# Attention beside a stream of projections: each block's values one block later, right behind the next block's turned weights

## The chip, the cores and the metric

The kernel runs on one core of a Trainium2 chip. The metric is device microseconds of one execution of the whole program; a figure for a kernel is the median over several executions. A profiled execution gives a trace as well, in which "span" is the time from the first to the last instruction of the program.

## What is computed

One layer of a hybrid trunk for 512 latent and 128 context tokens, 1024 features wide: a gated feed-forward half-step, then token mixing (differential attention beside a chunked recurrent memory), then a second feed-forward half-step, each under modulated norms. The change lies in the attention. Cut to that:

```python
def diff_attention(q, k, v, lam):          # 8 heads, blocks of 128 queries
    s = einsum('bqhcd,bkhcd->bhcqk', qi, kf) * scale     # c: two score maps per head
    pr = softmax(s, axis=-1)
    w = pr[:, :, 0] - lam * pr[:, :, 1]
    return einsum('bhqk,bkhv->bqhv', w, vf)              # then a norm per head
```

The four blocks of latent queries see 768 keys (512 latent, 256 cached); the one block of context queries sees its own 128.

## The kernel before

All weights and activations are 32-bit floats. The large products are made of three matmuls each, on operands split into a high and a low part (`mm3`). The program is built with a scheduler that orders the instructions of each engine at build time by its own estimates, unless the code pins them: matmuls and transposes always keep the order of the program (`mm` and `tr`, lines 74 to 78), and what stands under `with written():` (line 69) keeps its order on VectorE and ScalarE among what is pinned. Other instructions of VectorE and ScalarE are placed between the pinned ones by the scheduler.

The attention loop (lines 1961 to 2025) goes over 8 heads and, in each, over 5 blocks of 128 queries (`qi` 0 to 4; block 4 is the context's). Two things share TensorE there. One is the attention itself. The other is a queue of projection work (`fill`): units of 24 matmuls that belong to the memory branch or to later heads, of which the table `UNITS` (line 1954) gives each block one or two, and each head's end some more. Heads 0 and 1 mostly have two per block, the later heads mostly one. A unit's result is evacuated from PSUM by ScalarE (in some cases VectorE), unpinned. For the weights of a unit, ScalarE makes the high part (`fill.ahead`, pinned at the end of a block) and VectorE the low part (`fill.low`, pinned behind the scores' minimum).

A block consists of these steps, all pinned:

- `scores` (line 1597): up to eight matmuls into the one place for scores (`sc`, three PSUM banks, one buffer), then on VectorE the minimum of each row (`mn`, line 1617); queries carry a minus sign, so this is the soft-max's maximum.
- `soft` (line 1620): on ScalarE the exponentials of both maps, with their sums (`p0`, `p1`, `sm`). When they are read, the place for scores is free for the next block.
- `mix` (line 1628): on VectorE the reciprocals of the sums (`rc`, line 1631), a factor `r`, and the mixed weights, written over `p0` (in the profile `p<-p,r,p`).
- `turn` (line 1636): TensorE transposes of the mixed weights (`ps_wT`, six, or one in block 4), copied to SBUF (`wT`, two buffers) by ScalarE.
- `values` (line 1648): the product of the turned weights and the values (`ps_o`: twelve matmul instructions, two in block 4), evacuated by VectorE with the reciprocal as its scale (`ao`, line 1656).

`mn`, `sm`, `rc` and `wT` have two buffers each, and `p1` one. The other PSUM tiles (`ps_wT`, `ps_o`, the units' `ps_t` and `ps_p`, the turned queries and keys `ps_qkT`) share five banks. The order in a block is: scores of this block, turn of the block before, exponentials of this block, low part, first unit, mix of this block, values of the block before, second unit if there is one, high part. Behind the fifth block the head's end has turn 4, the turning of the next head's queries, units, values 4, the head's norm, and the turning of the next head's keys. Between the blocks the scheduler places what the unpinned parts leave on VectorE, above all the norm and rotation of the projected queries and keys for the next pair of heads (`qk_norm_rope`, line 1470: `rope`, `q_tok`, `k_tok` in the profile), which falls into the odd heads.

Of the kernel before, what the change touches and what calls it, by code (L numbers as in the profile page):

```python
# [7 lines left out]
F32 = mybir.dt.float32  # L8
# [23 lines left out]
def tile_trunk(ctx: ExitStack, tc: tile.TileContext, a: dict):  # L32
# [4 lines left out]
    def placed(ins):  # L37
        if as_written[0] is in_row:
            i = ins.ins
            if i.engine in in_row:  # L40
                tc.add_manual_dep(
                    i, in_row[i.engine].name, mybir.DependencyInfo(mybir.DependencyClass.NoSync, mybir.DependencyReason.DATA),
                    reason="written",
                )
            in_row[i.engine] = i
        elif as_written[0]:
            tc.keep_in_program_order(ins)
        return ins
# [19 lines left out]
    @contextmanager  # L68
    def written():
        was, as_written[0] = as_written[0], in_row  # L70
        yield
        as_written[0] = was

    def mm(*args, **kw):
        tc.keep_in_program_order(nc.tensor.matmul(*args, **kw))  # L75
# [1467 lines left out]
    class Head:  # L1543
# [53 lines left out]
        def scores(self, qi):  # L1597
            s = ps_s.tile([128, 1536], F32, tag="sc", name="sc")
            qs = slice(qi * 128, (qi + 1) * 128)
            qT, kH, kL = self.qT, self.kH, self.kL  # L1600
            for c in range(2):
                if qi < 4:
                    for k0, k1 in (((0, 512), (512, 768)) if c == 0 else ((0, 256), (256, 768))):
                        o = s[:, c * 768 + k0 : c * 768 + k1]
                        mm(o, qT[:, c, qs], kH[:, c, k0:k1], start=True, stop=False)
                        mm(o, qT[:, c, qs], kL[:, c, k0:k1], start=False, stop=True)
                else:

                    o = s[:, c * 512 : c * 512 + 256].rearrange("p (c t) -> p c t", c=2)
                    mm(o, qT[:, c, qs], kH[:, :, 768:896], start=True, stop=False)  # L1610
                    mm(o, qT[:, c, qs], kL[:, :, 768:896], start=False, stop=True)
            if qi < 4:
                sv = s.rearrange("p (c t) -> p c t", c=2)
            else:
                sv = s[:, 0:1280].rearrange("p (c t) -> p c t", c=2)[:, :, 0:128]
            mn, sm, rc = (ap.tile([128, 2], F32, tag=n, name=n, bufs=2) for n in ("mn", "sm", "rc"))
            placed(vec.tensor_reduce(out=mn, in_=sv, axis=AX.X, op=ALU.min))  # L1617
            self.s[qi] = sv, 768 if qi < 4 else 128, mn, sm, rc

# [66 lines left out]
    def begin_pools():  # L1686
        gates.close()
        in_pools["k"] = ctx.enter_context(tc.tile_pool(name="mlk", bufs=1, side="right"))
        in_pools["q"] = queries_of.enter_context(tc.tile_pool(name="mlq", bufs=1, side="right"))
# [21 lines left out]
    def load_memory(h):  # L1711
        for box, tag, src in ((mqT, "q", mq_dram), (mkT, "k", mk_dram)):
            box[h] = pair(tag, h, f"m{tag}T")
            nc.sync.dma_start(out=box[h], in_=src[:, 2 * h : 2 * h + 2, :])
# [209 lines left out]
    ap = att.enter_context(tc.tile_pool(name="att", bufs=1, reuse_waits="tile"))  # L1924
# [16 lines left out]
    def aside(hd, qi, part):  # L1941
        if hd == 0:
            for _ in range(ROWS.get((qi, part), 0)):
                next(rows, None)
        if part == 0:
            with written():
                fill.low()
        if part == 1 and hd == 1 and qi in (1, 2):
            gate_load(qi - 1)
        if part == 0 and hd == 1 and qi in (2, 3):  # L1950
            gate_cols()
# [9 lines left out]
    for hd in range(8):  # L1961
        H = heads[hd]
        odd = hd % 2
        for qi in range(5):
            n = UNITS[hd][qi]
            with written():
                H.scores(qi)
                if qi > 0:
                    H.turn(qi - 1)
                H.soft(qi)  # L1970
            aside(hd, qi, 0)
            fill.units(n[0])
            with written():
                H.mix(qi)
            if late is not None:
                late()
                late = None
            if qi > 0:
                with written():
                    H.values(qi - 1)  # L1980
            if qi == 3 and hd < 7:
                with written():
                    heads[hd + 1].pack()
            aside(hd, qi, 1)
            if (hd, qi) == (0, 2):
                begin_pools()
            elif (hd, qi) == (1, 0):
                load_memory(0)
            fill.units(n[1])
            with written():  # L1990
                fill.ahead()
        n = UNITS[hd][-1]
        with written():
            H.turn(4)
        if hd < 7:
            N = heads[hd + 1]
            N.queries()
            fill.units(n[0])
            with written():
                H.values(4)  # L2000
            H.finish_norm()
            if odd:
                for i in range(5):
                    fill.one()
                    if i in (0, 1):
                        N.keys(i)
                    if i == 1:
                        with written():
                            fill.ahead()
            else:  # L2010
                N.keys(0)
                fill.units(n[1])
                N.keys(1)
                with written():
                    fill.ahead()
                fill.units(n[2])
            late = H.finish
        else:
            fill.eager = True
            fill.units(1)  # L2020
            H.values(4)
            H.finish_norm()
            fill.drain(3)
            with written():
                H.finish()
# [511 lines left out]
def build(nc, shapes):  # L2537
    a = {}
    for n, s in shapes.items():
        a[n] = nc.dram_tensor("in_" + n, s, F32, kind="ExternalInput").ap()  # L2540
    for n, s in _OUTS.items():
        a[n] = nc.dram_tensor("out_" + n, s, F32, kind="ExternalOutput").ap()
    with tile.TileContext(nc, schedule_with_timeline_sim=True) as tc:
        tile_trunk(tc, a)
# [21 lines left out]
```

## Time and profile before

| | |
|---|---|
| median of 3 executions | 1815.26 us (1815.12 to 1816.54) |
| the profiled execution | 1815.7 us, span 1813.9 us |
| TensorE busy | 1785.6 us (98%) |
| VectorE busy | 1349.6 us (74%) |
| ScalarE busy | 910.8 us (50%) |
| attention loop, first scores to last values | 683.8 to 1071.0 us of the span |
| moved from and to HBM | 240.49 MB read, 68.87 MB written |

In the profile PE is TensorE (PEld its weight loads), DVE VectorE, ACT ScalarE, SP the queue that issues most DMAs. A row of the order of time has the start in us from the span's start, the duration in us, the engine, the line of the code, the operation, and what it writes and reads; at its end, in brackets, the idle time of the engine before it and what ended that. A row of the waits has who waited for whom, the total in us, how many times and the longest. A row of a stretch has its bounds and its length, the busy time of PE, PEld, DVE, ACT and POOL with their instructions, the granted clock of TensorE as a share of full speed, the share of the DMA engines and their GB/s. Matmuls are pipelined, and the end that a row gives for them overlaps the next one's start; the distance between two starts is what one costs.

### The profile page before, as it was taken

Reading aid. Unit: us, or ns where it says so; the run is one execution under the profiler, and the core shown is the slowest. Engines: PE = TensorE matmul, PEld = TensorE weight load, DVE = VectorE, ACT = ScalarE, POOL = GpSimd, SP = SyncE. Lnnn points to the kernel's source line nnn. Section 1 sums busy time; section 2 is a strip of 40 time slices with the busy share of each in tenths; the row PEclk is TensorE's granted clock in tenths of the full one; section 3 lists DMA queues with packets and bytes.
Section 4 is the critical chain, followed back from the end, with each engine's and each line's share of the span. In section 5 each row is a group of like instructions: output and inputs, shape, how many; then the busy total and the mean of one; then the engine's idle time right before and its main releaser. Section 6 shows DMA issues by size and latency. Waiting matters only on the chain.

```text
span 1813.9 us, 30780 instructions
## 1 busy us (share of the span) xinstructions
PE 1785.6 (98%) x12550; PEld 1744.6 (96%) x12550; DVE 1349.6 (74%) x2178; ACT 910.8 (50%) x1588; POOL 39.2 (2%) x69
## 2 busy tenths in 40 slices
PE   8999999999999999999999999999999999999998
PEld 6999999999999999999999998899999999999998
DVE  6879987677888765858584557977767888897485
ACT  5654544333655445556564547674336545554432
POOL 0000000100000000000000000000000000000010
PEclk9999999999999999999999999999999999999999
DMA  8355566977245434221221124576642355557992
GB/s 326 111 198 171 186 236 221 350 227 266 83 139 181 160 131 143 78 69 63 69 69 55 68 81 163 182 257 218 221 171 80 134 173 185 203 180 274 353 311 80
DMA packets 132207, 311.36 MB, mean 172 GB/s; under 512 B 10017, under 2 KB 93217, under 8 KB 119009
## 3 DMA queue, kind: packets, MB, share of 16 engines
q1 hardware_dynamic: 121122, 265.22, 42.3%
q0 software_dynamic: 10256, 41.55, 7.1%
q8 instruction: 98, 1.61, 0.4%
q10 hardware_dynamic: 688, 2.63, 0.4%
q14 instruction: 43, 0.35, 0.1%
HBM read 240.49 MB, written 68.87 MB: 171 GB/s over the span
## 4 chain that ended last, share of the span: by engine, by line
PE 85%; DVE 7%; DMA 4%; ACT 2%; issue 1%; SPq 0%; DVEq 0%; ACTq 0%
PE ps_f L75 48%; PE ps_p L75 14%; PE ps_t L75 12%; PE sc L75 2%; PE ps_n L75 2%; PE ps_o L75 2%; DVE ww L54 2%; PE ps_u L75 1%; DMA raw_a<-in_w_ada_k 1%; PE ps_wT L78 1%; PE ps_qkT L78 1%; DMA raw<-in_w2b 1%; DVE junk L814 1%; DMA P<-nm_dram 1%; DVE mn L1617 1%
## 5 line engine op out<-in xcount | busy, mean ns | idle before, releaser
L75 PE MATMUL ps_f<-S,ww 128*128 128x320 f32 x2400 | 387.5, 310 | 5.2 <-DVE ww L54 1.9
L75 PEld LDWEIGHTS ps_f<-S,ww 128*128 128x128 f32 x2400 | 359.8, 188 | 9.6 <-DVE ww L54 6.5
L54 DVE TENSOR_TENSOR ww<-raw,ww 128x2048 fp32r<-128x2048 f32 (+1 forms) x73 | 163.9, 2246 | 74.3 <-ACT ww L51 74.2
L75 PE MATMUL ps_t<-wH,hH 128*128 128x256 f32 x640 | 185.7, 290 | 0.9 <-DVE x L57 0.9
L75 PE MATMUL ps_f<-hm,ww 128*128 128x320 f32 x1176 | 185.8, 309 | 0.1
L75 PE MATMUL ps_t<-wH,hL 128*128 128x256 f32 x640 | 181.6, 284 | 0.9 <-DVE hL L54 0.9
L75 PE MATMUL ps_t<-wL,hH 128*128 128x256 f32 x640 | 181.4, 283 | 0.0
L75 PEld LDWEIGHTS ps_f<-hm,ww 128*128 128x128 f32 x1176 | 175.7, 188 | 0.6 <-DVE ww L54 0.6
L51 ACT ACTIVATE ww<-raw 128x2048 fp32r<-128x2048 f32 (+1 forms) x73 | 136.9, 1875 | 60.3 <-DVE raw L54 33.0
L54 DVE TENSOR_TENSOR raw<-raw 128x1024 f32<-128x1024 f32 x186 | 161.0, 865 | 2.2
L75 PE MATMUL ps_f<-hm,wB 128*128 128x320 f32 x1008 | 161.5, 309 | 0.0
L75 PE MATMUL ps_p<-hH,wH 128*128 128x320 f32 x480 | 151.1, 315 | 0.7 <-ACT aT L51 0.7
L75 PEld LDWEIGHTS ps_f<-hm,wB 128*128 128x128 f32 x1008 | 151.3, 188 | 0.0
L75 PE MATMUL ps_p<-hH,wL 128*128 128x320 f32 x480 | 148.3, 309 | 0.0
L75 PE MATMUL ps_p<-hL,wH 128*128 128x320 f32 x480 | 148.3, 309 | 0.0
L51 ACT ACTIVATE u<-ps_f 128x320 f32<-128x320 f32 x129 | 55.8, 433 | 161.5 <-PE ps_f L75 159.7
L75 PEld LDWEIGHTS ps_t<-wH,hH 128*128 128x128 f32 x640 | 123.0, 192 | 1.5 <-ACT nsq L51 1.1
L75 PEld LDWEIGHTS ps_t<-wH,hL 128*128 128x128 f32 x640 | 122.9, 192 | 1.1 <-DVE hL L54 1.1
L75 PEld LDWEIGHTS ps_t<-wL,hH 128*128 128x128 f32 x640 | 123.1, 192 | 0.4
L1617 DVE TENSOR_REDUCE mn<-sc 128x2 f32<-128x1536 f32 (+1 forms) x40 | 59.5, 1489 | 56.0 <-PE sc L75 55.8
L54 DVE TENSOR_TENSOR wB<-raw,wB 128x1024 fp32r<-128x1024 f32 x64 | 78.1, 1221 | 26.7 <-ACT wB L51 26.7
L51 ACT ACTIVATE wH<-raw 128x2048 fp32r<-128x2048 f32 (+1 forms) x45 | 75.4, 1681 | 42.2 <-PE ps_p L75 35.5
(309 smaller groups left out, 3621.9 us busy)
## 6 DMA issues: line engine op xcount, KB each, us to landing
g_dram<-g SPq DMA_DIRECT2D x44, 640.0 KB, 7.6
raw_a<-in_w_ada_c POOLq DMA_DIRECT2D x35, 512.0 KB, 4.7
g_dram<-g SPq DMA_DIRECT2D x24, 480.0 KB, 8.1
raw<-in_w1b SPq DMA_DIRECT2D x11, 1024.0 KB, 4.9
raw<-in_w3b SPq DMA_DIRECT2D x11, 1024.0 KB, 6.3
raw<-in_w1a SPq DMA_DIRECT2D x10, 1024.0 KB, 4.9
raw<-in_w3a SPq DMA_DIRECT2D x10, 1024.0 KB, 6.2
hm<-g_dram SPq DMA_DIRECT2D x7, 1280.0 KB, 12.5
```

Source lines behind the costliest of these rows:

```text
L51: return placed(nc.scalar.activation(*args, **kw))
L54: return placed(eng.tensor_tensor(out=out, in0=in0, in1=in1, op=op))
L75: tc.keep_in_program_order(nc.tensor.matmul(*args, **kw))
L78: tc.keep_in_program_order(nc.tensor.transpose(*args, **kw))
L814: placed(vec.tensor_tensor_reduce(out=junk, in0=raw, in1=self.csil[:, v, :], op0=ALU.mult, op1=ALU.add, scale=1.0, scalar=0.0, accum_out=m ...
L1617: placed(vec.tensor_reduce(out=mn, in_=sv, axis=AX.X, op=ALU.min))
```

## The change

Values move from behind the mix to right behind the turn, and one block further on. In block q the turn is that of block q-1, as before, and the values are now those of block q-2, and they stand ahead of the exponentials in the code, ahead of the first unit on TensorE, and ahead of the low part and the mix on VectorE. Blocks 0 and 1 have no values; the head's end has two: values 3 right behind turn 4, and values 4 where they were. `rc` gets a third buffer, because a block's reciprocals are still to be read when those of the second block after it get their place. Nothing else is changed.

```diff
@@ -1613,7 +1613,7 @@
-            mn, sm, rc = (ap.tile([128, 2], F32, tag=n, name=n, bufs=2) for n in ("mn", "sm", "rc"))
+            mn, sm, rc = (ap.tile([128, 2], F32, tag=n, name=n, bufs=b) for n, b in (("mn", 2), ("sm", 2), ("rc", 3)))
@@ -1967,6 +1967,8 @@
                 H.scores(qi)
                 if qi > 0:
                     H.turn(qi - 1)
+                if qi > 1:
+                    H.values(qi - 2)
                 H.soft(qi)
             aside(hd, qi, 0)
             fill.units(n[0])
@@ -1975,9 +1977,6 @@
             if late is not None:
                 late()
                 late = None
-            if qi > 0:
-                with written():
-                    H.values(qi - 1)
             if qi == 3 and hd < 7:
                 with written():
                     heads[hd + 1].pack()
@@ -1992,6 +1991,7 @@
         n = UNITS[hd][-1]
         with written():
             H.turn(4)
+            H.values(3)
         if hd < 7:
             N = heads[hd + 1]
             N.queries()
```

## The prediction

> **What bounds the kernel now.** I read the page's first part, then the waits of TensorE alone in the attention stage (683.8 to 1071.0 us of the span), then the order of time in the blocks whose order changes.
>
> ```profile
> span 1813.9 us, 30780 instructions
> ...
> PE 1785.6 (98%) x12550; PEld 1744.6 (96%) x12550; DVE 1349.6 (74%) x2178; ACT 910.8 (50%) x1588; POOL 39.2 (2%) x69
> ```
>
> ```profile
> 683.80:1071.00 387.20, 382.05 (x3043) 371.98 (x3042) 251.16 (x387) 215.27 (x454) 0.00 (x0) 1.00 0.22 74
> ```
>
> ```profile
> PE ps_wT L78 <- DVE p L57: 3.0, 7, 0.8
> PE sc L75 <- ACT p L51: 1.6, 3, 0.9
> PE ps_o L75 <- ACT wT L51: 0.5, 1, 0.5
> ```
>
> The second fence is the attention stage: length, then the busy time of TensorE, its weight loads, VectorE, ScalarE. The third is all that TensorE waits for there (total, times, longest). TensorE is the bound, in program order; of 387.2 us it idles 5.1. So an order that removes no TensorE work can win only out of those 5.1, and any cover that it takes from a wait shows in the time at once. Two of the three waits are the soft-max chain: the turn of a block waits for its mixed weights (`p`, DVE L57), and the next scores wait until the exponentials (ACT) have read the one place for scores. Only the third concerns the values.
>
> **What the change moves.** No instruction is added or removed. Between the scores of block q and the turn of q, TensorE had: turn q-1, a unit of the projections, values q-1, scores q+1. Afterwards it has turn q-1, values q-2, the unit, scores q+1. For q from 2 on that is the same amount of cover, and block 0 never had values. For q = 1 there is no q-2: twelve matmuls of cover go, and they come back behind turn 4, where the head's end has units and turned queries to spare. So the price lies in the second block of each head. Head 2, its second block:
>
> ```profile
> 799.64 0.20 ACT L51 ACTIVATION_READ_ACCUMULATOR p<-sc,mn 128x1 f32 x1
> ...
> 799.89 0.50 PE L75 MATMUL sc<-kH,qT 128*128 128x512 f32 x1 [0.34 <-ACT p L51]
> ...
> 801.40 0.87 PE L78 MATMUL ps_wT<-ident,p 128*128 128x128 f32 x6
> ...
> 802.03 0.36 PE L75 MATMUL ps_t<-wH,hH 128*128 128x256 f32 x1
> ...
> 804.99 1.50 PE L75 MATMUL ps_o<-v_tok,wT 128*128 128x128 f32 x12
> 805.08 0.20 ACT L51 ACTIVATION_READ_ACCUMULATOR p<-sc,mn 128x1 f32 x1
> ...
> 805.93 1.02 DVE L57 SCALAR_TENSOR_TENSOR p<-p,r,p 128x768 f32<-128x768 f32 x1
> 806.25 0.47 PE L75 MATMUL sc<-kH,qT 128*128 128x512 f32 x1
> ...
> 807.73 0.82 PE L78 MATMUL ps_wT<-ident,p 128*128 128x128 f32 x6
> ```
>
> The values' twelve matmuls hold TensorE from 804.99 to 806.25: **1.26 us**. Without them the scores of block 2 want to start at 804.99, but the exponentials are read out at 805.08 + 0.20 = 805.28; the rows at 799.64 and 799.89 show scores starting 0.05 behind such an end, so 805.33. From there scores to turn takes 801.40 - 799.89 = 1.51 (that case too began with a wait): 806.84. The mixed weights end at 805.93 + 1.02 = 806.95, and the turn follows an end of the mix by 0.05 (head 3 below: 851.36 + 1.02 = 852.38, turn at 852.43): 807.00. Free of waits the turn would come at 807.73 - 1.26 = 806.47. Lost: **0.53**. In short: the new turn is at the mix's end + 0.05, the old turn less 1.26 is what it should be. Heads 4, 6 and 7, mix and old turn:
>
> ```profile
> 900.26 1.02 DVE L57 SCALAR_TENSOR_TENSOR p<-p,r,p 128x768 f32<-128x768 f32 x1
> ...
> 902.08 0.81 PE L78 MATMUL ps_wT<-ident,p 128*128 128x128 f32 x6
> ...
> 1000.47 1.02 DVE L57 SCALAR_TENSOR_TENSOR p<-p,r,p 128x768 f32<-128x768 f32 x1
> ...
> 1002.21 0.82 PE L78 MATMUL ps_wT<-ident,p 128*128 128x128 f32 x6
> ...
> 1048.96 1.02 DVE L57 SCALAR_TENSOR_TENSOR p<-p,r,p 128x768 f32<-128x768 f32 x1
> ...
> 1050.85 0.82 PE L78 MATMUL ps_wT<-ident,p 128*128 128x128 f32 x6
> ```
>
> Head 4: 901.33 against 900.82, **0.51**. Head 6: 1001.54 against 1000.95, **0.59**. Head 7: 1050.03 against 1049.59, **0.44**. Heads 0 and 1 run two units in this block; one unit is 804.99 - 802.03 = 2.96 more cover, so nothing is lost. In heads 3 and 5 the turn waits for the mix already:
>
> ```profile
> 849.12 1.48 DVE L1475 TENSOR_REDUCE ss<-rope 128x20 f32<-128x1280 f32 x1
> ...
> 851.36 1.02 DVE L57 SCALAR_TENSOR_TENSOR p<-p,r,p 128x768 f32<-128x768 f32 x1
> ...
> 852.43 0.87 PE L78 MATMUL ps_wT<-ident,p 128*128 128x128 f32 x6 [0.31 <-DVE p L57]
> ...
> 943.83 0.23 ACT L51 ACTIVATION_READ_ACCUMULATOR p<-sc,mn 128x1 f32 x1
> ...
> 944.16 0.47 PE L75 MATMUL sc<-kH,qT 128*128 128x512 f32 x1
> ...
> 946.24 0.34 DVE L61 TENSOR_SCALAR ao<-ps_o,rc 128x128 f32<-128x128 f32 x1
> 946.38 0.87 PE L78 MATMUL ps_wT<-ident,p 128*128 128x128 f32 x6 [0.58 <-DVE p L57]
> 946.50 0.17 DVE L57 SCALAR_TENSOR_TENSOR rt<-ry 128x20 f32<-128x20 f32 x1
> ...
> 958.61 0.17 DVE L1631 RECIPROCAL rc<-sm 128x2 f32<-128x2 f32 x1 [1.33 <-ACT p L51]
> ```
>
> Nothing there ends the mix earlier, so the whole **1.26** is lost in each. Sum of the second blocks: 0.53 + 0.51 + 0.59 + 0.44 + 2 x 1.26 = **4.59**.
>
> VectorE's order changes as well: the evacuation `ao` stood behind the mix, now it stands behind the scores' minimum and ahead of the weights' low part (`fill.low`) and the mix; the wait that it adds is for the moved values, and low part, reciprocals and mix are queued behind it. Where no low part follows, VectorE would wait for the exponentials then anyway, and `ao` costs nothing; where one follows, the mix is late, which matters only where it is tight, in head 7, block 3:
>
> ```profile
> 1057.76 0.82 PE L78 MATMUL ps_wT<-ident,p 128*128 128x128 f32 x6
> ...
> 1059.63 2.28 DVE L54 TENSOR_TENSOR wL<-raw,wH 128x2048 fp32r<-128x2048 f32 x1
> ...
> 1061.94 1.50 PE L75 MATMUL ps_o<-v_tok,wT 128*128 128x128 f32 x12
> ...
> 1062.28 1.02 DVE L57 SCALAR_TENSOR_TENSOR p<-p,r,p 128x768 f32<-128x768 f32 x1
> ...
> 1063.47 0.35 DVE L61 TENSOR_SCALAR ao<-ps_o,rc 128x128 f32<-128x128 f32 x1 [0.17 <-PE ps_o L75]
> ...
> 1063.74 0.82 PE L78 MATMUL ps_wT<-ident,p 128*128 128x128 f32 x6
> ```
>
> `ao` starts 1.53 behind its first matmul (1061.94 to 1063.47). The turn before it, at 1057.76, takes 0.63 (801.40 to 802.03), so `ao` comes at 1059.92 and the low part at about 1060.2, 0.57 late; the mix ends at 1063.87, the turn at 1063.92 in place of 1063.74: **0.18**. For the other side, in heads 3 and 5 VectorE works almost without a break, and `ao` takes 0.26 there between mix and next minimum (946.24 to 946.50). One of these now falls where VectorE sat idle (1.33 ahead of 958.61). Bounds: nothing, or 0.35 in each of three blocks of both heads, 2.1; I take 0.26 in each head, **-0.5**, the nearer to a VectorE that is full.
>
> The values' own wait (0.5, in head 7's last block) goes, but the next instruction, turn 4, waits for its mix regardless: nothing. The third place for `rc` is the condition of the order, not a cost: its 8 bytes live one block longer. No DMA is issued in the moved lines; in SP's queue nothing changes place. POOL has no instruction here.
>
> Sum: 4.59 + 0.18 - 0.5 = **4.3 us**. The profiled execution took 1815.7 (span 1813.9 and 1.8 around it), so 1820.0 on its footing; it stood 0.4 over the median of 1815.26, so on the median's footing **1819.6 us**, 0.24% more.
>
> **Rivals.** *VectorE's order is dealt anew (not slower).* The rotation of the next heads' queries and keys isn't pinned; its place in VectorE's stream is chosen when the program is built. In heads 3 and 5 the 1.48 us reduction at 849.12 stands ahead of the mix. If it goes behind it, the mixes end up to 1.48 earlier, and the exponentials bound these blocks: in head 5 the scores start at 943.83 + 0.23 + 0.05 = 944.11 and the turn 1.51 later, 945.62 against 946.38 - 1.26 = 945.12, a loss of 0.5; as much in head 3 at most, 1.0 together in place of 2.52. With such slack the late waits of head 5 go too:
>
> ```profile
> 958.63 0.39 PE L75 MATMUL sc<-kH,qT 128*128 128x256 f32 x1 [0.90 <-ACT p L51]
> ...
> 960.14 1.26 PE L78 MATMUL ps_wT<-ident,p 128*128 128x128 f32 x6 [0.78 <-DVE p L57]
> ```
>
> ```profile
> 957.06:960.47 3.41, 1.73 (x13) 1.34 (x13) 2.01 (x6) 3.41 (x8) 0.00 (x0) 1.00 0.12 38
> 960.47:963.88 3.41, 3.41 (x18) 3.41 (x17) 2.28 (x6) 2.07 (x7) 0.00 (x0) 0.50 0.00 0
> ```
>
> The column before the DMA share is the granted clock: after a stretch with TensorE busy for 1.73 of 3.41 it was 0.50 for 3.41 us, which costs half of that, 1.7. Gain: 1.48 of the 0.90 + 0.78, and 1.7. Total 2.07 + 1.0 + 0.18 - 0.5 - 1.48 - 1.7 = -0.4: **1814.8**, no change that can be measured. It decides from mixes over 1 us earlier. For it: the order is open. Against: the minima and mixes are pinned, and the reduction was ready early. Chance 0.18.
>
> *The clock drops (slower).* In the second blocks of heads 3 and 5 the new idle time and the old lie within some 3.5 us: for head 5, 944.11 less 942.90 (944.16 - 1.26) ahead of the scores, 1.21, and 946.38 - 945.62 = 0.76 ahead of the turn, 2.0 in all; as the rows show, TensorE idled 1.7 ahead of 960.47. Two more half-rate stretches give 4.3 + 3.4: **1823.0**. The chance, 0.12, is small because it hangs on where a stretch begins. The Trainium skill (TensorE: Matmul & The Clock Gate, Part 1) has the half rate come only after a whole idle window of about 3.4 us; by that rule this rival is out and the sum stays 4.3. The trace does not agree: no wait ahead of 960.47 is over 0.90.
>
> *The head's end pays back.* The values behind turn 4 cover the copies of the turned weights, which they wait on today. At most twice 0.5 comes back: 4.3 - 1.0 = **1818.6**. Against: only one such wait is in the list, and not at a head's end with queries. Chance 0.08. That the order stays as it was can't be: matmuls and transposes are kept in program order.
>
> **How the numbers follow.** A measurement of this kernel can tell 0.2%, 3.6 us, from no change. Forecast 0.62, of which 0.12 lies below 3.6 us (an uncertain -0.5 to -2.1, and the unpinned work). Slower: 0.50 + 0.12 = 0.62. Same: 0.12 + 0.08 + 0.15 of the first rival = 0.35. Faster: the 0.03 left of it. The range goes from the first rival's 1814.8 to a little over the clock's 1823.0, 1823.2.
>
> **What would show it.** Right: TensorE's waits in the stage grow from 5.1 to some 9 us, the growth stands at the second blocks, as waits of `sc` for the exponentials (three of about 0.3 in heads 2, 4, 6, more in 3 and 5) and of `ps_wT` for `p`; values never wait for `wT`. Wrong: the same waits at an unchanged total, mixes of heads 3 and 5 that end over 1 us sooner behind their scores, or a stage that grew without TensorE waiting.

## The result and the profile after

| | before | after |
|---|---|---|
| median | 1815.19 us (6 executions, 1813.88 to 1816.54) | 1821.53 us (6 executions, 1820.46 to 1822.88) |
| profiled execution | 1815.7 us, span 1813.9 us | 1820.95 us, span 1819.2 us |

The ratio is 1.0037 (95% interval 1.0026 to 1.0047): slower by 6.3 us in the medians, and the interval does not contain 1. The forecast was 4.3 us (1819.6, range 1814.8 to 1823.2), a little under the 4.7 us at which the interval begins. The sign, and the place of the larger part, were right; some 2 to 3 us were not in the sum.

The first part of the page after:

```profile
span 1819.2 us, 30753 instructions
...
PE 1786.7 (98%) x12550; PEld 1744.3 (96%) x12550; DVE 1351.0 (74%) x2178; ACT 910.7 (50%) x1588; POOL 39.2 (2%) x69
```

The attention stage after, from first scores to last values, as one stretch (length, busy TensorE, weight loads, VectorE, ScalarE), and all waits of TensorE from 680 to 1085 us:

```profile
683.58:1075.87 392.29, 382.57 (x3041) 369.95 (x3040) 252.68 (x386) 215.28 (x453) 0.00 (x0) 1.00 0.22 73
```

```profile
PE ps_wT L78 <- DVE p L57: 6.1, 7, 1.4
PE sc L75 <- ACT p L51: 2.9, 8, 1.0
PE ps_wT L78 <- ACT mqT L51: 0.5, 1, 0.5
```

The same engines do the same work, and the stage is 392.29 us; before, up to the same instruction, it was 386.87 us (683.77 to 1070.64; the prediction's 387.20 runs a little further). TensorE's waits went from 5.1 to 9.5 us. The new ones are those that the prediction named: five more waits of the scores for the exponentials, and twice as much time of the turns waiting for the mixed weights. Values no longer wait for `wT`. A single wait of 0.5, for ScalarE's copy of a unit (`mqT`) at the end of head 6, was not named; before, the same turn waited 0.36 there for its mix.

Head 2, its second block, in the order of time; these rows answer to those of before at 804.99 to 807.73:

```profile
801.86 0.40 PE L75 MATMUL sc<-kL,qT 128*128 128x512 f32 x1
...
805.76 0.20 ACT L51 ACTIVATION_READ_ACCUMULATOR p<-sc,mn 128x1 f32 x1
806.02 0.50 PE L75 MATMUL sc<-kH,qT 128*128 128x512 f32 x1 [0.19 <-ACT p L51]
806.35 0.39 PE L75 MATMUL sc<-kL,qT 128*128 128x512 f32 x1
...
806.62 1.02 DVE L57 SCALAR_TENSOR_TENSOR p<-p,r,p 128x768 f32<-128x768 f32 x1
...
807.06 0.40 PE L75 MATMUL sc<-kH,qT 128*128 128x512 f32 x1
807.30 0.40 PE L75 MATMUL sc<-kL,qT 128*128 128x512 f32 x1
807.70 0.87 PE L78 MATMUL ps_wT<-ident,p 128*128 128x128 f32 x6
```

Where twelve matmuls stood, the scores now wait for the exponentials (805.76 + 0.20 = 805.96), and the turn follows the mix's end (806.62 + 1.02 = 807.64) by 0.06. After the last scores of the block, which began at 801.86, the turn comes 5.84 us later; in the same block of head 6 it comes 5.83 later, in head 7 6.33. The forecast was built on just this.

The profile of before has a half-rate stretch of the clock in head 5, that of after has none in this stage. A second profile of before (the experiment `e10_before_again` below) has none there either; its stage is 385.35 us. Beside that one, after is 392.29 - 385.35 = **6.94 us** longer, which agrees with 6.3 from the medians. Head by head, from the start of a head's first scores to that of the next head's, against that second profile (the columns of experiments belong to the next section):

| head | forecast | after | e5 | e9 | e1 | e2 | e6 |
|---|---|---|---|---|---|---|---|
| 0 | 0 | 0.03 | 0.00 | 0.01 | 0.01 | 0.03 | 0.03 |
| 1 | 0 | 0.82 | 0.24 | 0.23 | -0.01 | 0.56 | 0.83 |
| 2 | 0.53 | 0.66 | 0.79 | 0.82 | 0.65 | 0.67 | 0.67 |
| 3 | 1.26 - 0.26 | 2.22 | 1.55 | 1.56 | 1.01 | 2.23 | 0.73 |
| 4 | 0.51 | 0.67 | 0.83 | 0.81 | 0.67 | 0.66 | 0.69 |
| 5 | 1.26 - 0.26 | 0.60 | 2.88 | 1.41 | -0.57 | 0.49 | 0.60 |
| 6 | 0.59 | 0.87 | 0.78 | 0.14 | 0.72 | 0.78 | 0.87 |
| 7 | 0.44 + 0.18 | 1.06 | 0.66 | 0.17 | 0.62 | 0.66 | 1.09 |
| sum | 4.3 | 6.9 | 7.7 | 5.2 | 3.1 | 6.1 | 5.5 |

Head 5 of e5 has a half-rate stretch in its profile, which was worth 1.5 in before (head 5 there is 1.53 longer in the first profile than in the second), so e5 stands at about 6.2. Heads 2, 4, 5, 6 and 7 of after are forecast within 0.45. What the sum lacked is head 3 (+1.2) and head 1 (+0.8).

In head 3 it is the fourth block. VectorE and the turn there, before:

```profile
862.39 1.22 DVE L54 TENSOR_TENSOR q_tok<-q_tok,rope 128x1024 f32<-128x1024 f32 x1
...
863.77 0.49 DVE L1720 COPY mkT<-ps_p 128x320 f32<-128x320 f32 x1 [0.16 <-PE ps_p L75]
864.41 0.17 DVE L1631 RECIPROCAL rc<-sm 128x2 f32<-128x2 f32 x1 [0.16 <-ACT p L51]
...
866.04 0.84 PE L78 MATMUL ps_wT<-ident,p 128*128 128x128 f32 x6 [0.50 <-DVE p L57]
```

and after:

```profile
863.68 1.22 DVE L54 TENSOR_TENSOR q_tok<-q_tok,rope 128x1024 f32<-128x1024 f32 x1
...
864.81 0.34 DVE L61 TENSOR_SCALAR ao<-ps_o,rc 128x128 f32<-128x128 f32 x1
865.70 0.17 DVE L1631 RECIPROCAL rc<-sm 128x2 f32<-128x2 f32 x1 [0.55 <-ACT p L51]
866.46 0.49 DVE L1720 COPY mkT<-ps_p 128x320 f32<-128x320 f32 x1 [0.59 <-PE ps_p L75]
...
867.11 1.02 DVE L57 SCALAR_TENSOR_TENSOR p<-p,r,p 128x768 f32<-128x768 f32 x1
...
868.28 0.85 PE L78 MATMUL ps_wT<-ident,p 128*128 128x128 f32 x6 [1.38 <-DVE p L57]
```

`mkT` is the evacuation of this block's projection unit, one of the few that VectorE makes, and it is not pinned: the scheduler put it ahead of the factor `r`. Before, the unit stood ahead of the values on TensorE, and its result was there 1.38 us after the rotation's last step had begun (863.77 - 862.39). Now the values stand ahead of the unit, its result is there 2.78 us behind that step's start (866.46 - 863.68), 1.40 later, and `r` and the mix, which have nothing to do with it, are queued behind it: VectorE waits 0.59 for the unit, and the turn 1.38 in place of 0.50.

### The profile page after: what moved, and what is told of

Read it like the earlier page. It is cut to its first block, busy times and chain, and to the rows that moved or that the text cites. A ratio compares the mean times of both kernels' runs of the same rounds, so it can differ in the third digit from the quotient of the medians.

```text
span 1819.2 us, 30753 instructions
## 1 busy us (share of the span) xinstructions
PE 1786.7 (98%) x12550; PEld 1744.3 (96%) x12550; DVE 1351.0 (74%) x2178; ACT 910.7 (50%) x1588; POOL 39.2 (2%) x69
## 4 chain that ended last, share of the span: by engine, by line
PE 84%; DVE 7%; DMA 5%; ACT 3%; issue 1%; SPq 0%; DVEq 0%; ACTq 0%
PE ps_f L75 47%; PE ps_p L75 14%; PE ps_t L75 11%; PE ps_o L75 2%; PE sc L75 2%; DVE ww L54 2%; PE ps_n L75 1%; DMA raw_a<-in_w_ada_k 1%; PE ps_wT L78 1%; PE ps_qkT L78 1%; DMA P<-nm_dram 1%; PE ps_u L75 1%; DMA raw<-in_w2b 1%; DVE junk L814 1%; ACT p L51 1%
## 5 line engine op out<-in xcount | busy, mean ns | idle before, releaser
L54 DVE TENSOR_TENSOR ww<-raw,ww 128x2048 fp32r<-128x2048 f32 (+1 forms) x73 | 163.9, 2245 | 73.1 <-ACT ww L51 73.0
L54 DVE TENSOR_TENSOR raw<-raw 128x1024 f32<-128x1024 f32 x186 | 160.7, 864 | 2.2
L54 DVE TENSOR_TENSOR wB<-raw,wB 128x1024 fp32r<-128x1024 f32 x64 | 78.0, 1219 | 25.8 <-ACT wB L51 25.8
```

The lines of the kernel that those rows point to most:

```text
L54: return placed(eng.tensor_tensor(out=out, in0=in0, in1=in1, op=op))
```

## The experiments

My theory after the result: the loss is the second block's cover, as forecast, and what lies beyond it is VectorE's order in the blocks behind it (the unit's copy in head 3, `ao` ahead of the mix elsewhere). Its rivals: that `ao`'s place is the cost all over; that the place next to the turn is; that the second block's loss runs on into later blocks whatever the order; and, for the head's end, that its work is spare and could serve as cover.

**e1: only the first block's values later.** The order of before, but block 0's values stand in block 2, ahead of those of block 1 (and `rc` has three places).

```diff
-            if qi > 0:
+            if qi > 1:
                 with written():
+                    if qi == 2:
+                        H.values(0)
                     H.values(qi - 1)
```

> The kernel before, with one thing moved: values 0 of each head run in block 2 (behind its mix, ahead of values 1) in place of block 1, with three places for rc. All other values and all evacuations stay where they were. Theory of the lost cover: block 1 loses 1.26 us of TensorE work in heads 2 to 7, 4.6 us in all, so about 1819.8 us, with the second blocks' turns at 5.83 us behind the last scores in heads 2, 4 and 6 as in the changed kernel. Rival, VectorE's order (the evacuation ahead of the mix and the re-dealt unpinned work is what costs): within 1 us of the kernel before, since that order is nearly untouched.

Measured: 1818.44 us (11 executions, 1815.88 to 1819.96) beside 1815.84 of before, ratio 1.0013 (1.0004 to 1.0022). In the second blocks the loss is there as forecast (0.65 to 0.72 in heads 2, 4 and 6), but the total is lower than the 4.6 expected: in block 2 twice the cover now stands, and it took away waits that before had behind it: ahead of the turn of block 3 in head 3 0.16 in place of 0.50, and in head 5 0.06 in place of the 0.90 and 0.78 (head 5 is 0.57 shorter). So the cover that goes in block 1 has a price, and cover put into block 2 has a value; this experiment mixes the two, and e9 parts them.

**e2: `ao` behind the mix.** The changed kernel, with the evacuation of the values taken out of `values` and put behind the mix.

```diff
+            self.s[qi] = p, rc
+
+        def scaled(self, qi):
+            p, rc = self.s.pop(qi)
             ts(self.ao[:, qi, :], p, rc[:, 0:1], ALU.mult)
...
+            if qi > 1:
+                with written():
+                    H.scaled(qi - 2)
```

> The changed kernel, with only the evacuation of the values (ao) put back behind the mix of the same block; the matmuls of the values stay behind the turn, one block late. Lost cover: the second blocks still lose their 4.6 us; what VectorE's order costs in heads 1, 3 and 7 (about 2 us) comes back in part, so 1819.5 to 1820.5 us. VectorE's order: almost all of the 6.3 us comes back, 1815 to 1816.5 us.

Measured: 1822.97 us (5 executions, 1819.95 to 1825.63), ratio to before 1.0039 (1.0027 to 1.0052), as slow as after, where 1 to 2 us were expected back. By the profiles 0.26 comes back in head 1 and 0.40 in head 7, nothing in head 3. VectorE of e2 there:

```profile
866.44 0.17 DVE L1631 RECIPROCAL rc<-sm 128x2 f32<-128x2 f32 x1 [0.81 <-ACT p L51]
867.29 0.49 DVE L1724 COPY mkT<-ps_p 128x320 f32<-128x320 f32 x1 [0.69 <-PE ps_p L75]
867.70 0.21 DVE L57 SCALAR_TENSOR_TENSOR r<-sm,nlam,rc 128x1 f32<-128x1 f32 x1
```

`ao` no longer stands there, and the copy waits all the same. By the profiles the place of `ao` is worth 0.85 us in the stage, and the medians don't show it; as the cause of the whole loss it is out.

**e3 and e4: more cover in the second block.** One of the units at the ends of heads 2, 4, 5 and 6 goes into their second block; in e3 in the changed kernel, in e4, as a control, in the kernel before.

```diff
-        2: (one,) * 5 + ((1, 1, 1),), 3: (two, one, one, one, one, (0,)),
-        4: (one,) * 5 + ((1, 1, 1),), 5: (two, one, one, one, one, (1,)),
-        6: (two, one, one, one, one, (1, 1, 1)), 7: (two, one, one, one, (0, 0), (0, 0)),
+        2: (one, two, one, one, one, (1, 1, 0)), 3: (two, one, one, one, one, (0,)),
+        4: (one, two, one, one, one, (1, 1, 0)), 5: (two, two, one, one, one, (0,)),
+        6: (two, two, one, one, one, (1, 1, 0)), 7: (two, one, one, one, (0, 0), (0, 0)),
```

> The changed kernel, with the last unit of the end of heads 2, 4, 5 and 6 run in block 1 of the same head, a second unit there. The computation and the order of the queue of units are the same. Lost cover: the waits of block 1 in these four heads go, 0.66 + 0.66 + 0.87 + 1.2 us by the trace, so about 3.3 us under the changed kernel, near 1818 us. VectorE's order: no change, 1821.5 us, as no instruction of the attention on VectorE moves.

> Control: the kernel before with the same four units moved into block 1. Lost cover: heads 2, 4 and 6 had no wait there, head 5 one of 0.6 to 0.7 us, so 0 to 0.7 us faster, about 1814.7 us; what e3 gains beyond this is cover that the change took away. A theory by which an extra unit in block 1 is good in itself has it as much faster as e3 is against the changed kernel.

Measured: e3 1829.51 us (5 executions, 1827.33 to 1832.87), ratio to before 1.0077 (1.0063 to 1.0091); e4 1836.46 us (4 executions, 1833.01 to 1838.11), ratio 1.0109 (1.0095 to 1.0123). Both expectations missed by far. The waits of the second blocks in heads 2, 4 and 6 did go (the turn there comes over 8.0 us behind the last scores, without a wait), but other waits came. TensorE's list in e3, then in e4:

```profile
PE ps_wT L78 <- DVE p L57: 10.3, 7, 2.6
PE sc L75 <- ACT kL L51: 2.8, 3, 2.0
```

```profile
PE ps_aT L78 <- DVE ao L54: 7.5, 2, 3.7
PE ps_wT L78 <- DVE p L57: 5.0, 7, 1.3
PE sc L75 <- ACT kL L51: 2.7, 3, 2.0
PE ps_o L75 <- ACT wT L51: 2.4, 4, 0.9
```

The units at a head's end cover its norm (`ao`, L54, and the turns `ps_aT` behind it), the next head's keys (`kL`) and, in the last block, the mix. So these units were not spare where they stood. That e3 is less slow than e4, though after is slower than before, fits with values 3 of the changed order covering something at that end; which part of the 7 us between them it makes is not settled.

**e5: the delay alone.** Values one block later, as in the change, but at their old place, behind the unit and the mix.

```diff
                     H.turn(qi - 1)
-                if qi > 1:
-                    H.values(qi - 2)
                 H.soft(qi)
...
+            if qi > 1:
+                with written():
+                    H.values(qi - 2)
```

> The changed kernel, with the values (one block late, as changed) put back to their old place within the block: behind the first unit and the mix, matmuls and evacuation both. So the block is one later, and nothing stands next to the turn. Lost cover: block 1 of heads 2 to 7 loses its 1.26 us as in the changed kernel, while the units stay where the kernel before has them within the block, so head 3's block 3 (0.9 us) and head 7's last blocks (0.5 us) come back: 1 to 2 us under the changed kernel, about 4.5 us over the kernel before. If the place next to the turn is what costs: within 1 us of the kernel before.

Measured: 1822.38 us (6 executions, 1819.76 to 1825.07) beside 1815.30 of before, ratio 1.0039 (1.0026 to 1.0053). The delay by a block costs as much without the new place as with it, and more than the 4.5 expected here (6.2 by the profile, with the half-rate stretch taken off). The profiles show what the place does: at the old place head 3 is 0.67 cheaper (the unit ends as early as before, and the turn of its fourth block comes 6.87 behind its scores, as in before), head 1 0.58 and head 7 0.40 cheaper, and head 5, with its stretch taken off, 0.8 dearer. So the place has a price in three heads and a gain in one (and 0.15 in heads 2 and 4).

**e6: the unit's copy on the other engine.** The changed kernel, with the evacuations `mkT` of all four units of this kind in head 3, the one above among them, on ScalarE.

```diff
-    keys_of_memory(1)
+    keys_of_memory(1, by_act=True)
```

> The changed kernel, with the memory's keys of head 1 evacuated by ScalarE in place of VectorE (the units that run in blocks 1 to 4 of attention head 3). If the rest of head 3's loss is a copy on VectorE that waits for its unit, which now ends later, ahead of the mix: the wait of 1.38 us ahead of head 3's turn 3 falls to about 0.5 and the head is some 0.9 us shorter. If it is only the lost cover of block 1: that wait stays over 1.2 us.

Measured, one execution: 1821.76 us, no less than after; what lies outside the attention stage differs by more than the effect between single executions (the stage begins at 686.25 here, at 683.58 in after). The profile is read head by head: head 3 is 0.73 over before in place of 2.22, and no other head moves by more than 0.03. TensorE's waits, and the block in question:

```profile
PE ps_wT L78 <- DVE p L57: 4.3, 6, 1.2
```

```profile
867.60 0.17 DVE L1631 RECIPROCAL rc<-sm 128x2 f32<-128x2 f32 x1 [0.55 <-ACT p L51]
867.80 0.22 DVE L57 SCALAR_TENSOR_TENSOR r<-sm,nlam,rc 128x1 f32<-128x1 f32 x1
868.06 1.02 DVE L57 SCALAR_TENSOR_TENSOR p<-p,r,p 128x768 f32<-128x768 f32 x1
...
869.14 0.88 PE L78 MATMUL ps_wT<-ident,p 128*128 128x128 f32 x6
```

One wait and 1.5 us are gone from that head: the copy behind the displaced unit is what the sum lacked there. That it is 1.5 and not the 0.88 by which the wait had grown has two reasons. The whole wait went, the 0.50 that before had there with it: no wait stands ahead of the turn at 869.14. And the edit moves more than the one copy: another had stood ahead of the second block's mix, and the turn behind that mix waits 0.60 in place of 1.00. About 0.3 is lost again at the head's end.

**e7: values of the same block right behind their turn.** The order of before without any delay: turn and values of block q-1 next to each other.

```diff
                     H.turn(qi - 1)
+                    H.values(qi - 1)
                 H.soft(qi)
...
-            if qi > 0:
-                with written():
-                    H.values(qi - 1)
```

> The kernel before, with the values of block q-1 right behind turn q-1 in block q: next to the turn, but in the same block. No cover is lost in any block. If the block's delay is what the place next to the turn needs, TensorE waits in nearly each of the 31 full blocks for ScalarE's copies of the turned weights, some 0.6 us each: 15 to 20 us slower. If the copies are early enough, no change.

Measured, one execution: 1855.13 us, some 40 over before. Expected were 15 to 20; the direction is right, the size is not. The wait that the change's delay avoids, and the clock around the first of its longest cases:

```profile
PE ps_o L75 <- ACT wT L51: 25.1, 34, 2.1
```

```profile
759.82:763.23 3.41, 1.55 (x12) 1.17 (x11) 2.43 (x2) 3.41 (x5) 0.00 (x0) 1.00 0.00 0
763.23:766.64 3.41, 3.41 (x18) 3.41 (x18) 1.72 (x4) 2.15 (x7) 0.00 (x0) 0.50 0.00 0
```

The values wait 34 times for ScalarE's copies of the turned weights, longest where other ScalarE work (a weight's high part, 1.9 us) stands ahead of them. Four half-rate stretches lie in the stage, at some 1.7 us each (an estimate, half of 3.41) 6.8 together: three right behind waits of values of 1.86 us and more, one behind a turn's wait of 1.97 for its mix. A fourth wait of values of 1.86, at 968.80, has none behind it. So values need work between themselves and their turn; before has a unit there, the change a whole block.

**e8: the other end of e1.** The order of before, with the values of block 1 in heads 1, 3 and 5 moved from block 2 to block 3, where TensorE waited.

```diff
-            if qi > 0:
+            if qi > 0 and (hd, qi) not in ((1, 2), (3, 2), (5, 2)):
                 with written():
+                    if (hd, qi) in ((1, 3), (3, 3), (5, 3)):
+                        H.values(1)
                     H.values(qi - 1)
```

> The kernel before, with values 1 of heads 1, 3 and 5 run in block 3 (ahead of values 2) in place of block 2, and three places for rc. Lost cover read the other way: block 2 of these heads has 0.7 us and more to spare (turns at 7.28, 7.66 and 11.21 us against mixes at 6.54, 6.55 and 7.39), and block 3 has TensorE waiting 0.44, 0.66 and 2.0 us. So heads 1 and 3 gain about 0.5 us each, head 5 0.7 us and the half-rate stretch behind it where there is one (1.7 us): 1.7 to 3 us faster than the kernel before. If the order on VectorE were what counts, no change, or slower by a mix that comes later.

Measured: 1815.20 us (12 executions, 1811.56 to 1816.34), ratio 0.9995 (0.9986 to 1.0005): no difference that can be told, where 1.7 to 3 us less were expected. The stage is 1.4 us shorter in the profile, 0.5 in head 1, 0.3 in head 3 and 0.6 in head 5. In heads 3 and 5 cover went from a block where it was needed too: the turn of block 2 now stands at the mix. With VectorE full there, moving TensorE's work about moves the wait. The third place for `rc` is not what costs: e8 has it and is not slower, and e9, which has two, is. No version here is measurably faster than before.

**e9: only the second block's cover taken away.** The order of before without the first block's values in the second block. In their place the last block does block 3's product twice, and block 0's rows get the second of them, so that the work is the same, the result for block 0 is left out, and blocks 2 and 3 have the cover that they had before.

```diff
-            if qi > 0:
+            if qi > 1:
                 with written():
+                    if qi == 4:
+                        H.s[0] = H.s[3]
                     H.values(qi - 1)
+                    if qi == 4:
+                        H.values(0)
```

> The kernel before, with only the second block's values taken away: that block has none, and the fifth block does the product of the fourth block's turned weights twice, the second time in place of block 0's (so block 0's rows get block 3's result). The amount of work is the same, the blocks 2 and 3 have the order and the cover that they had before, and no second values stand in block 2. Theory A (the loss is the second block's cover, worked out as 4.59 us, and what the changed kernel lost beyond it is VectorE's order in blocks 2 to 4): 4.6 us over before, less up to 0.7 where the fifth block's new cover meets head 7's wait there: 3.9 to 4.6, a ratio of 1.0021 to 1.0025; head by head +0.5 to +0.7 in heads 2, 4, 6 and 7, about +1.3 in heads 3 and 5, nothing in 0 and 1; the turn of block 3 in head 3 keeps its wait of 0.5. Theory B (the second block's loss runs on into the blocks behind it whatever their order): as slow as the changed kernel, some 6 us, with +2.2 in head 3 and the wait of its turn 3 grown to 1.4, since the unit whose copy stands there ends 1.26 later here too.

Measured: 1818.97 us (10 executions, 1816.29 to 1823.11) beside 1814.78 of before, ratio 1.0027 (1.0018 to 1.0037), 4.9 us (4.2 in the medians); by the profiles 5.16. The turn of block 3 in head 3 comes 6.87 us behind its scores, as in before, so the loss does not run on, and theory A holds there; the medians alone would not part A from B's 6 us. The time is a little over A's 3.9 to 4.6, though head 6 lost less than expected (0.14): the wait of 0.36 ahead of its last turn is covered here. The excess stands in heads 2, 3, 4 and 1, at 0.2 to 0.3 each. In heads 2 and 4 half of it is the size of the term (next section), and half lies at the head's end, where the turning of the next queries takes 1.05 in place of 0.90.

**e10: before, once more.**

> The kernel before, unchanged, for a second profile: it shows whether the stretch of 3.41 us at half rate in head 5 of the first profile belongs to the order or comes and goes. Theory A (it comes and goes): head 5 is about 1.7 us shorter, and all other heads agree with the first profile within 0.15 us, so that head-by-head differences of 0.5 us can be read from single profiles. Theory B (it belongs to the waits of 0.90 and 0.78 there): the stretch is there again behind these waits. TensorE's waits in the attention stage: 5.1 us in either case, within 0.3.

Measured, one execution: 1815.02 us. Head 5 is 1.53 shorter than in the first profile, all other heads agree within 0.02. The half-rate stretch of before belongs to one execution, not to the order, and single profiles can be read head by head to some hundredths. In this second profile the same waits of head 5 (0.90 and 0.78) lie in two stretches of 3.41 us, not in one:

```profile
956.75:960.16 3.41, 2.55 (x23) 2.36 (x21) 2.10 (x2) 2.16 (x6) 0.00 (x0) 1.00 0.11 38
960.16:963.57 3.41, 2.59 (x20) 2.39 (x21) 3.32 (x7) 3.41 (x9) 0.00 (x0) 1.00 0.00 0
```

The bounds are those of the grid on which half-rate stretches lie (see the last section), carried on from the only one of this profile before its end, at 35.16 us: here TensorE was busy for 2.55 and 2.59 of 3.41 and the clock stayed, in the first profile for 1.73 and it fell.

## Why the prediction was right, and where not

**The second block's cover: right.** "The new turn is at the mix's end + 0.05, the old turn less 1.26 is what it should be" gave turns 5.83 us behind the last scores in heads 2 and 6 and 6.33 in head 7, and these were measured within 0.01. e9, where nothing but this cover goes, costs 4.9 us by the ratio (3.3 to 6.7) against the forecast's 4.59. Heads 0 and 1, with two units there, lose nothing in that block, as said.

**"The old turn less 1.26": too small a size.** The term of the second blocks is 0.1 to 0.3 too low per head (0.66 for 0.53, 0.67 for 0.51, 0.87 for 0.59). Up to the turn it is exact: in head 2 this turn comes 12.43 us behind the head's first scores, before (second profile) 13.15, so 0.54 of the 1.26 are lost. What was mis-sized is the cover. Where nothing waits, in heads 0 and 1, the turn of this block comes 1.32 and 1.34 sooner, not 1.26, since a change of group on TensorE goes with the values. The first scores matmul right behind values takes 0.32 to the next, with no wait, where the same shape inside its group takes 0.24 (807.06 to 807.30). Before:

```profile
806.25 0.47 PE L75 MATMUL sc<-kH,qT 128*128 128x512 f32 x1
806.57 0.39 PE L75 MATMUL sc<-kL,qT 128*128 128x512 f32 x1
```

Another 0.06 is the turn: right behind the end of its mix it takes 0.71 to the next group (807.70 to 808.41), with its mix done before, 0.65 (in the next block). With both, head 2 comes to 0.53 + 0.08 + 0.06 = 0.67, and head 4 to 0.65. Head 6 comes to 0.73, and the rest is the wait at its end, 0.53 in place of 0.36. In heads 3 and 5 the whole cover is lost, so there too it is 1.34 and not 1.26.

The list of waits, 9.5 against 5.1, shows only 4.4 of the 6.9 us. It counts from the modelled end of the matmul before and so shows too little: the scores at 806.02 are listed with 0.19, but the unit's last matmul began at 805.55, 0.47 ahead, where 0.12 is usual, so the wait costs 0.35. The turn at 807.70 also came late, 0.40 behind the last scores where 0.23 is usual, and is listed with no wait at all.

**"For q from 2 on that is the same amount of cover": true, and not enough.** This is the step that failed. I counted the cover between scores and turn, which keeps its length, and not who reads the things in it. The unit ends some 1.3 later against its block's scores, its evacuation stands on VectorE ahead of the mix in head 3, and the rows there show `r` and the mix start only behind it. Of head 3's 2.22, 1.33 is the second block's cover and 0.89 the turn behind this mix. e5 and e9, where the unit stands ahead of the values, don't have the 0.89 (the turn is at 6.87, as before), and e6 shows it by removal (2.22 to 0.73, with all four copies gone). The prediction looked for what is queued behind `ao`, the instruction that moves, and not behind the evacuation of the unit that it displaces.

**"Where no low part follows ... `ao` costs nothing": mostly right.** In head 7's fourth block `ao` ahead of the low part made the turn late as forecast (0.18). It fails in head 7's last block, which the prediction didn't look at: there the values, which `ao` waits for, end no sooner than the exponentials. VectorE there, after:

```profile
1069.62 0.35 DVE L61 TENSOR_SCALAR ao<-ps_o,rc 128x128 f32<-128x128 f32 x1 [1.83 <-PE ps_o L75]
1069.89 0.15 DVE L1631 RECIPROCAL rc<-sm 128x2 f32<-128x2 f32 x1
1070.08 0.22 DVE L57 SCALAR_TENSOR_TENSOR r<-sm,nlam,rc 128x1 f32<-128x1 f32 x1
1070.33 0.35 DVE L57 SCALAR_TENSOR_TENSOR p<-p,r,p 128x128 f32<-128x128 f32 x1
...
1070.74 0.33 PE L78 MATMUL ps_wT<-ident,p 128*128 128x128 f32 x1 [1.16 <-DVE p L57]
```

The exponentials end at 1069.62 (ScalarE), when `ao` starts, so `rc` comes 0.27 behind them, before 0.03. They end late themselves, since the turn of the fourth block was late and the copies of its weights stand ahead of them on ScalarE. The turn waits 1.16. In e2, with `ao` behind the mix, head 7 is 0.40 cheaper and head 1 0.26.

**VectorE's relief, -0.5: half right.** I took 0.26 in each of heads 3 and 5. Head 5 got more (0.60 lost where the cover is 1.34, so some 0.7 back: the scores of its last block wait 0.20 in place of 0.90), head 3 none that can be seen beside the copy. By e5 against after the new place is what gives it in head 5 (0.8).

**"The head's end has units and turned queries to spare": wrong as a general claim, harmless in the sum.** Taking four units from there cost 8 us in the changed kernel (e3) and 21 us in the kernel before (e4). The change only adds to that end, and nothing in the sum rested on a gain there. The rival that it pays back (-1.0) did not happen: no such wait stood there, as its own counter-argument said.

**The other rivals.** VectorE's order was dealt anew in places, but against the kernel: in head 1's fourth block a step of the rotation (0.42 long) moved behind the minimum and, with `ao`, the turn is 0.6 later; no mix came over 1 us sooner. The clock didn't drop in the stage of after in its profile, though it came near: the stretch of its second block in head 3 has TensorE busy for 2.06 of 3.41.

```profile
850.77:854.18 3.41, 2.06 (x12) 1.55 (x13) 3.38 (x7) 0.73 (x4) 0.00 (x0) 1.00 0.72 245
```

What stays open is the cause of a part of head 1's 0.82. By place, 0.60 is this turn in its fourth block, of which `ao` is 0.26 (e2), and 0.25 lies in its third block, where the load of a unit's weights behind the values waits 0.22 for ScalarE's copy of the turned weights. At the old place (e5, e9) the third block loses nothing and the fourth block's turn is still 0.4 later; the step of the rotation was not tried by itself.

## What to carry to other kernels

Take the size of a group's cover from the starts around it, with the group and without it: here 1.34 us, where the group's own rows gave 1.26. A matmul group that moves on TensorE also displaces what it moves past. Before counting cover as equal, list for every displaced group who reads its result, on which engine that reader stands, and what is queued behind it there: here a copy of 0.49 us that nobody waits for held the soft-max chain. And work that lies between a wait and its cause is not spare because no wait is seen there; take it away in an experiment (with a control on the kernel before) ahead of calling it free.

## What the hardware showed unexpectedly

The half-rate stretches lie on a grid. In e7 they begin at 763.23 and 865.63, 102.40 us apart, which is 30 times 3.413, and each lasts 3.41 us. Cut by that grid, the eleven half-rate stretches in the attention stages of these traces come right behind a stretch in which TensorE was busy for at most 1.74 of 3.41 us, about half, and all with 2.03 or more are followed by full rate. From e3:

```profile
825.96:829.37 3.41, 1.01 (x9) 0.81 (x7) 3.37 (x7) 2.13 (x10) 0.00 (x0) 1.00 0.45 132
829.37:832.78 3.41, 3.22 (x17) 3.25 (x17) 2.25 (x6) 1.37 (x3) 0.00 (x0) 0.50 0.43 180
870.33:873.74 3.41, 2.03 (x17) 1.85 (x16) 2.80 (x6) 2.54 (x5) 0.00 (x0) 1.00 0.00 0
```

Outside of the attention stages the edge is not so clean: 1.65 us busy was followed by full rate (before, 31.97 to 35.38), 1.93 by half rate (e5, 30.80 to 34.21). What counts as busy for the clock was not tried, and the busy time is modelled. The same waits cost 1.5 us or nothing by where the grid falls, which differs between executions (head 5 of before in its two profiles, 1.53 apart). The Trainium skill (TensorE: Matmul & The Clock Gate, Part 1) gives a free-running window of 3413 ns, and the traces agree with that. Its table has the half rate come after an idle window; that such a window is needed the traces don't bear out, since windows half busy brought it.
